# Row means by one fused VectorE instruction, and a small early load on ScalarE's queue, in a subtract-mean-and-square kernel

## The chip, the cores and the metric

One core of a Trainium2 chip. The metric is device time in microseconds (us) of one execution; the six runs of the changed kernel lie within 0.3% of each other (82.98 to 83.23).

## The reference

```python
x = np.random.randn(1024, 4096).astype(np.float32)      # axis = -1
mean = np.mean(x, axis=axis, keepdims=True)
return ((x - mean) ** 2).astype(np.float32)
```

16.78 MB are read and 16.78 MB are written.

## The kernel before

The 1024 rows are cut into two tiles. A tile has 128 partitions with four rows of 4096 fp32 each, so a partition's run is 64 KiB. All loads are issued at once, a tile is worked on in place, and one store writes it back.

```python
Q = 4
HEAD = 512
H = D * 9 // 16                                   # 2304
...
cuts = [0, HEAD, Q * D] if i == 0 else [0, Q * D]  # first tile: 2 KiB a row, then the rest
for lo, hi in zip(cuts, cuts[1:]):
    nc.sync.dma_start(out=x_tile[:, lo:hi], in_=x_t[i][:, lo:hi])
...
for i in range(ntiles):
    row = [tiles[i][:, q * D:(q + 1) * D] for q in range(Q)]
    m3 = mean_on_act(row[3])       # one ScalarE pass with accum_out
    m0 = mean_on_dve(row[0])       # reduce_sum over 4096, then a 128x1 scaling
    square_on_act(row[3], m3)
    m1 = mean_on_dve(row[1])
    square_on_act(row[0], m0)
    m2 = mean_on_dve(row[2])
    square_on_act(row[1], m1)
    square_on_act(row[2][:, :H], m2)
    back = row[2][:, H:]           # the last 1792 elements on VectorE
    nc.vector.tensor_scalar_add(out=back, in0=back, scalar1=m2)
    nc.vector.tensor_mul(out=back, in0=back, in1=back)
    nc.sync.dma_start(out=out_t[i], in_=tiles[i])
```

## Time and profile before

| what | value | how to read it |
|---|---|---|
| time | 83.23 us, median of three (83.11 to 84.35) | one of three runs was 1.3% longer |
| span of the profile | 81.4 us | the time without what lies around the program |
| VectorE, ScalarE busy | 33.4 us, 34.7 us | about 17 us for each tile |
| one large packet on each engine | 2.41 us | 1.049 MB over all 16, so 435 GB/s |
| landing of a tile to issue of its store | 17.02 us | 22.54 to 39.56 us |

The profile books the bytes of a transfer in bursts: all 16 DMA engines start a packet of 62 or 64 KiB within 0.7 us of each other in the kernel before (1.016 or 1.049 MB a burst). I give a burst's time as the mean over its bytes, from stretches of 0.05 us. The distance between two bursts is the yardstick of this document: 2.34 us within 62 KiB packets, 2.41 to 2.42 us within 64 KiB packets. Anything longer I count as lost. I call the place where the last load ends and the first store begins the first joint.

### The profile page before, as it was taken

To read this page: it belongs to the slowest core of one execution; us is meant where nothing else is said; L and a number is where in the kernel's file an instruction comes from. 1 tells how busy PE (TensorE), PEld (TensorE's weight loads), DVE (VectorE), ACT (ScalarE), POOL (GpSimd) and SP (SyncE) were. 2 spreads that over 40 slices of the span, in tenths; PEclk is the share of its full clock that TensorE was granted. 3 is DMA by queue.
4 is the path that set the end of the run, shared out by engine and by line. 5 is a ranking of instruction groups with operands and counts; after the bars stand their busy time and mean duration, and the time that the engine had idled before them with its cause. 6 is when DMAs were issued, how large, how long until landed. Compare 5 with 4: busy or idle time off the path is not lost.

```text
span 81.4 us, 83 instructions
## 1 busy us (share of the span) xinstructions
DVE 33.4 (41%) x16; ACT 34.7 (43%) x13; POOL 0.2 (0%) x4
## 2 busy tenths in 40 slices
DVE  0000000000089999999439999999900000000000
ACT  6000000000099999999339999999800000000000
POOL 0000000000000000000000000000000000000000
DMA  1999939999992999993899998399999199999290
GB/s 26 602 499 468 406 156 468 499 499 499 516 451 97 483 516 516 516 483 161 387 516 516 516 483 387 161 516 516 516 516 451 64 516 516 516 516 483 129 419 0
DMA packets 720, 33.55 MB, mean 412 GB/s; under 512 B 80, under 2 KB 80, under 8 KB 208
## 3 DMA queue, kind: packets, MB, share of 16 engines
q1 hardware_dynamic: 720, 33.55, 95.9%
HBM read 16.78 MB, written 16.78 MB: 412 GB/s over the span
## 4 chain that ended last, share of the span: by engine, by line
DMA 49%; DVE 21%; SPq 1%; issue 0%
DMA x_tile<-in_x_dram 49%; DVE neg_sum L67 16%; DVE x_tile L90 2%; DVE x_tile L89 1%; SPq L51 1%; DVE neg_mean L70 1%
## 5 line engine op out<-in xcount | busy, mean ns | idle before, releaser
L67 DVE TENSOR_REDUCE neg_sum<-x_tile 128x1 f32<-128x4096 f32 x6 | 26.5, 4412 | 25.0 <-DMA x_tile<-in_x_dram 25.0
L74 ACT ACTIVATE x_tile<-x_tile,neg_mean 128x4096 f32<-128x4096 f32 (+1 forms) x8 | 26.0, 3324 | 0.1
L59 ACT ACTIVATE copy<-x_tile 128x4096 f32<-128x4096 f32 x2 | 7.2, 3617 | 23.1 <-DMA x_tile<-in_x_dram 23.1
L90 DVE TENSOR_TENSOR x_tile<-x_tile 128x1792 f32<-128x1792 f32 x2 | 4.1, 2026 | 0.1
L89 DVE TENSOR_SCALAR x_tile<-x_tile,neg_mean 128x1792 f32<-128x1792 f32 x2 | 2.3, 1153 | 0.1
L59 ACT ACT_TABLE_LOAD x1 | 1.3, 1283 | 0.7 <-PEq L108 0.7
L70 DVE TENSOR_SCALAR neg_mean<-neg_sum 128x1 f32<-128x1 f32 x6 | 0.9, 154 | 0.2
L59 ACT ACTIVATION_READ_ACCUMULATOR copy<-x_tile 128x1 f32 x2 | 0.4, 186 | 0.0
L108 POOL MEMSET const-bfloat16-1.0<- 128x1 bf16 x1 | 0.1, 102 | 0.0
L108 POOL MEMSET const-uint8-127<- 128x1 uint8 x1 | 0.1, 101 | 0.0
L108 POOL MEMSET const-float32-0.0<- 128x1 f32 x1 | 0.1, 99 | 0.2 <-issue 0.2
L108 POOL MEMSET const-float32-1.0<- 128x1 f32 x1 | 0.1, 98 | 0.0
## 6 DMA issues: line engine op xcount, KB each, us to landing
x_tile<-in_x_dram SPq DMA_DIRECT2D x1, 7936.0 KB, 21.4
x_tile<-in_x_dram SPq DMA_DIRECT2D x1, 256.0 KB, 2.6
out_dram<-x_tile SPq DMA_DIRECT2D x2, 21.7
x_tile<-in_x_dram SPq DMA_DIRECT2D x1, 40.2
```

Of the source, the lines that this page charges most:

```text
L51: nc.sync.dma_start(out=x_tile[:, lo:hi], in_=x_t[i][:, lo:hi])
L59: nc.scalar.activation(out=copy, in_=row, func=ACT.Identity, scale=-inv_d, accum_out=neg_mean)
L67: inorder(nc.vector.reduce_sum(out=neg_sum, in_=row, axis=mybir.AxisListType.X, negate=True))
L70: inorder(nc.vector.tensor_scalar_mul(out=neg_mean, in0=neg_sum, scalar1=inv_d))
L74: inorder(nc.scalar.activation(out=part, in_=part, func=ACT.Square, bias=neg_mean, scale=1.0))
L89: nc.vector.tensor_scalar_add(out=back, in0=back, scalar1=m2)
L90: nc.vector.tensor_mul(out=back, in0=back, in1=back)
L108: nc = _bacc.Bacc("TRN2", target_bir_lowering=False, num_devices=1)
```

## The change

Its intent: fewer VectorE and ScalarE passes for the row means, and 256 KiB of the second tile loaded at the very start, on a second queue, while the first queue is only getting going. The diff, without the removed helper functions:

```diff
-    H = D * 9 // 16
+    HALF = D // 2
+    LAST = D - D // 8
...
-        cuts = [0, HEAD, Q * D] if i == 0 else [0, Q * D]
-        for lo, hi in zip(cuts, cuts[1:]):
-            nc.sync.dma_start(out=x_tile[:, lo:hi], in_=x_t[i][:, lo:hi])
+        if i == 0:
+            nc.sync.dma_start(out=x_tile[:, :HEAD], in_=x_t[i][:, :HEAD])
+            nc.sync.dma_start(out=x_tile[:, HEAD:], in_=x_t[i][:, HEAD:])
+        else:
+            end = Q * D - HEAD
+            nc.scalar.dma_start(out=x_tile[:, end:], in_=x_t[i][:, end:])
+            nc.sync.dma_start(out=x_tile[:, :end], in_=x_t[i][:, :end])
...
+        for q in range(Q):
+            row = tiles[i][:, q * D:(q + 1) * D]
+            pairs = scratch.tile([P, HALF], F32)
+            neg_mean = stats.tile([P, 1], F32)
+            inorder(nc.vector.tensor_tensor_reduce(
+                out=pairs, in0=row[:, :HALF], in1=row[:, HALF:],
+                scale=-inv_d, scalar=0.0, op0=ADD, op1=ADD, accum_out=neg_mean,
+            ))
+            cut = D if q < Q - 1 else LAST
+            nc.scalar.activation(
+                out=row[:, :cut], in_=row[:, :cut],
+                func=ACT.Square, bias=neg_mean, scale=1.0,
+            )
+            if cut < D:
+                rest = row[:, cut:]
+                nc.vector.tensor_scalar_add(out=rest, in0=rest, scalar1=neg_mean)
+                nc.vector.tensor_mul(out=rest, in0=rest, in1=rest)
```

More of the change, by code (lines that the diff above doesn't have):

```diff
@@ L12 @@
 ACT = mybir.ActivationFunctionType
+ADD = mybir.AluOpType.add
 @with_exitstack
@@ L43 @@
     scratch = ctx.enter_context(tc.tile_pool(name="scratch", bufs=1))
-    stats = ctx.enter_context(tc.tile_pool(name="stats", bufs=2 * ntiles * Q))
+    stats = ctx.enter_context(tc.tile_pool(name="stats", bufs=ntiles * Q))
     tiles = []
@@ L52 @@
         tiles.append(x_tile)
     inorder = tc.keep_in_program_order
-    def mean_on_act(row):
-        copy = scratch.tile([P, D], F32)
-        neg_mean = stats.tile([P, 1], F32)
-        nc.scalar.activation(
-            out=copy, in_=row, func=ACT.Identity, scale=-inv_d, accum_out=neg_mean
-        )
-        return neg_mean
-    def mean_on_dve(row):
-        neg_sum = stats.tile([P, 1], F32)
-        neg_mean = stats.tile([P, 1], F32)
-        inorder(nc.vector.reduce_sum(
-            out=neg_sum, in_=row, axis=mybir.AxisListType.X, negate=True
-        ))
-        inorder(nc.vector.tensor_scalar_mul(out=neg_mean, in0=neg_sum, scalar1=inv_d))
-        return neg_mean
@@ L73, in square_on_act @@
-    def square_on_act(part, neg_mean):
-        inorder(nc.scalar.activation(
-            out=part, in_=part, func=ACT.Square, bias=neg_mean, scale=1.0
-        ))
-    for i in range(ntiles):
-        row = [tiles[i][:, q * D:(q + 1) * D] for q in range(Q)]
-        m3 = mean_on_act(row[3])
-        m0 = mean_on_dve(row[0])
-        square_on_act(row[3], m3)
-        m1 = mean_on_dve(row[1])
-        square_on_act(row[0], m0)
-        m2 = mean_on_dve(row[2])
-        square_on_act(row[1], m1)
-        square_on_act(row[2][:, :H], m2)
-        back = row[2][:, H:]
-        nc.vector.tensor_scalar_add(out=back, in0=back, scalar1=m2)
-        nc.vector.tensor_mul(out=back, in0=back, in1=back)
+    for i in range(ntiles):
+        for q in range(Q):
[3 more added lines that the diff above has]
+            inorder(nc.vector.tensor_tensor_reduce(
+                out=pairs,
+                in0=row[:, :HALF],
+                in1=row[:, HALF:],
+                scale=-inv_d,
+                scalar=0.0,
+                op0=ADD,
+                op1=ADD,
+                accum_out=neg_mean,
+            ))
+            cut = D if q < Q - 1 else LAST
+            nc.scalar.activation(
+                out=row[:, :cut],
+                in_=row[:, :cut],
+                func=ACT.Square,
+                bias=neg_mean,
+                scale=1.0,
+            )
[3 more added lines that the diff above has]
+                nc.vector.tensor_mul(out=rest, in0=rest, in1=rest)
```

## The prediction

Two rates in it can be set beside the traces. ScalarE's 0.833 ns an element: before, its squares took 3698 ns for 4096 elements and 2200 ns for 2304, which is 0.836 ns. VectorE's 1 / 0.96 ns a pair: the plain tensor_tensor took 2026 ns for 1792 pairs before and 692 ns for 512 in the changed kernel, which is 1.042 ns; the two passes over those 512 elements took 0.49 and 0.69 us.

> **What bounds the kernel now.** I read the page's busy lines first. They rule out the engines: VectorE and ScalarE are each busy for about 34 us of 81.4, and both are empty for the first 22 and the last 22 us. The DMA line and the queue line point to the transfers.
>
> ```profile
> DVE 33.4 (41%) x16; ACT 34.7 (43%) x13; POOL 0.2 (0%) x4
> GB/s 26 602 499 468 406 156 468 499 499 499 516 451 97 483 516 516 516 483 161 387 516 516 516 483 387 161 516 516 516 516 451 64 516 516 516 516 483 129 419 0
> q1 hardware_dynamic: 720, 33.55, 95.9%
> ```
>
> The reader is to see one queue whose packets take 95.9% of sixteen engines' span. The dips in the GB/s row look like pauses. To settle that I cut time into 0.05 us stretches: the bytes come in bursts, one packet of 62 or 64 KB on each engine at once, 2.34 us apart in the first tile and 2.41 us apart after it, without a break from 2.7 to 77.4 us. I take the bytes to be booked when a packet starts, since the second tile's first burst (21.8 us) comes before the first tile has landed (22.5); the dips are then slices that fall between bursts. One packet per engine is 64 KiB x 16 = 1.049 MB; over 2.41 us that is 435 GB/s.
>
> The next views are the table by stretches, at the start and at the two joints (first load, second load, first store and second store follow each other on one queue), and the order of time around the first joint.
>
> ```profile
> 0.00:1.70 1.70, 0.00 (x0) 0.97 (x1) 0.20 (x4) 1.00 0.00 0
> 1.70:2.60 0.90, 0.00 (x0) 0.31 (x1) 0.00 (x0) 1.00 0.79 209
> 2.60:3.10 0.50, 0.00 (x0) 0.00 (x0) 0.00 (x0) 1.00 5.64 2179
> ...
> 38.30:39.20 0.90, 0.90 (x1) 0.90 (x1) 0.00 (x0) 1.00 2.70 1165
> 39.20:40.90 1.70, 0.30 (x1) 0.09 (x1) 0.00 (x0) 1.00 0.00 0
> 40.90:41.70 0.80, 0.00 (x0) 0.00 (x0) 0.00 (x0) 1.00 3.04 1311
> ...
> 77.20:77.90 0.70, 0.00 (x0) 0.00 (x0) 0.00 (x0) 1.00 3.45 1498
> ```
>
> ```profile
> 0.73 1.33 SPq L51 DMA_DIRECT2D x_tile<-in_x_dram  x3
> 22.54 3.62 ACT L59 ACTIVATE copy<-x_tile 128x4096 f32<-128x4096 f32 x1 [20.52 <-DMA x_tile<-in_x_dram]
> 22.61 4.42 DVE L67 TENSOR_REDUCE neg_sum<-x_tile 128x1 f32<-128x4096 f32 x1 [22.61 <-DMA x_tile<-in_x_dram]
> 26.28 13.01 ACT L74 ACTIVATE x_tile<-x_tile,neg_mean 128x4096 f32<-128x4096 f32 x4
> 37.47 2.03 DVE L90 TENSOR_TENSOR x_tile<-x_tile 128x1792 f32<-128x1792 f32 x1
> 39.56 19.64 SPq L91 DMA_DIRECT2D out_dram<-x_tile  x2
> 41.90 3.62 ACT L59 ACTIVATE copy<-x_tile 128x4096 f32<-128x4096 f32 x1 [2.61 <-DMA x_tile<-in_x_dram]
> ```
>
> The last load burst has its mean at 38.71 us and the first store burst at 41.16: 2.45 us, against 2.41 inside a transfer. The first store was issued at 39.56 and its first packets start near 41.0, about 1.45 us later. The second joint is the same (issue 58.9 us, burst 2.42 after the one before). So nothing is lost at either joint, and compute of 17.02 us a tile (22.54 to 39.56) is hidden under a transfer of 19.3 us. The margin is thin: at most 1.45 us between issue and first packet is needed and 1.45 us is there.
>
> The chain of waits says 49% DMA and 21% VectorE. Its VectorE part is the second tile's compute before the last store, but that store could not have started moving before the queue had drained at 60.4 us. Shortening that part alone buys nothing.
>
> The floor: first packets at 1.70 us, 33.55 MB at 435 GB/s is 77.1 us, and from the end of the last packet (77.4 + 2.4 = 79.8) to the span's end 1.6 us: 80.4 us against 81.4. At most 1.0 us, 1.2%, can be won by anything that leaves the bytes as they are. It lies between 1.7 and 2.6 us, where the first small load moves its 256 KiB at 209 GB/s, in 1.0 us instead of the 0.6 that the full rate would need, and in the spread of the engines.
>
> [...]
>
> **The change part by part.**
>
> The row means. Out go, per tile, three reductions of 4.41 us with a 0.15 us scaling each, and one ScalarE pass of 3.62 + 0.19 us. In come four instructions over two halves. By the trace, 2048 pairs at the tensor_tensor rate take 2026 + 256 / 0.96 = 2293 ns. Each is followed by a separate read of the accumulator, which I put at 0.15 to 0.19 us, after the tiny 0.15 us scaling and ScalarE's 0.19 us accumulator read. With a semaphore hop a row mean takes about 2.5 us, so VectorE needs 10.0 us for four.
>
> The squares. Now all on ScalarE but for 512 elements. Inside the group of four, starts are (13.01 - 2.20) / 3 = 3.60 us apart; the last, of 3584 elements, takes 2200 + 1280 x 0.833 = 3267 ns. Three starts and the last are 14.1 us. VectorE's 512 elements, about 0.5 + 0.7 us, come at 10 to 11.5 us and are hidden.
>
> So a tile's path from landing to store issue is first mean 2.5 + squares 14.1 + starts and semaphore 0.15 = 16.75 us, against 17.02: 0.27 us shorter, off the path. One trap: in the instruction order of the changed program the table load no longer runs at 0.7 us; it waits for the first tile. It takes 1.28 us while VectorE works on the first mean (2.5 us), so it is hidden[...].
>
> The early load. ScalarE's queue issues 256 KiB of the second tile at about 0.73 us, beside the first small load on the other queue. These bytes would cost 0.60 us at the full rate later, and that is saved. What they cost early is the question: if the engines fill the idle half of 1.7 to 2.6 us with them, big packets begin 0.1 to 0.2 us later and 0.4 to 0.5 us is won. If [...] each small packet keeps its 1.0 / 8 = 0.125 us of engine time, big packets begin 0.4 to 1.0 us later and the gain is from +0.2 to -0.4 us. I take a gain g of 0.2.
>
> The joint. The first tile now lands behind 256 KiB more: 22.54 + 0.6 - g = 22.94. Store one is issued at 22.94 + 16.75 = 39.69, while the queue drains at 41.1 - 0.2 = 40.9. If the issue really needs 1.45 us its packets start at 41.14 and 0.2 us is lost; if it needs the 0.97 us of the first load (issue 0.73, packets 1.70), nothing. I take 0.1 lost. At the second joint the tile lands earlier and compute is shorter, so there is no loss.
>
> Sum: 83.23 - 0.2 + 0.1 = 83.13. I say 83.1.
>
> **The rivals.** First, the half rate of the fused instruction. 2048 pairs would take about 4.4 us, a mean 4.65, and four 18.6. The last row's square could not begin before 18.6 us and would end at 21.9, so store one is issued at about 22.94 + 21.9 = 44.8 and the queue idles about 5 us at the first joint. The second tile hides most of its own delay behind the shifted store, so 88 us in all, plus 6%. [...] I give it 10%.
>
> Second, the early load only moves a cost[...]. Then 83.2 to 83.6. For it: 209 GB/s with small packets. A quarter.
>
> Third, the early load fills the hole wholly and nothing is lost at the joint: 82.7 to 82.9. A third.
>
> Fourth, faster compute shows in full, as the chain of waits with its 21% VectorE would suggest: 0.27 us or more. Against: 2.42 us at the joint, no gap to close.
>
> **Range and chances.** The middle cases give 82.7 to 83.6. One of three runs of before was 84.35, so a median can be off by some tenths; I take 82.3 to 84.2. Faster than 81.6 would need more than the whole 1.0 us: 2%. Slower than 84.9 is the half rate, with a little for what a second queue may add before the span: 9%. Within 2%: 89%.
>
> **What would show it.** Bursts 2.41 us apart through both joints, and the first large burst near 2.9 rather than 2.7 us: g is then 0.6 minus that shift. The fused instruction near 2.29 us, with a short accumulator read. Landing to store issue near 16.75 us. ScalarE's table load near 22.9 us and its first square waiting for VectorE. The prediction is wrong if the fused instruction is well over 3 us, if a burst distance at a joint is above 2.7 us, or if the first large burst comes later than 3.4 us.

## The result, and the profile after

The changed kernel takes 83.12 us (median of six, 82.98 to 83.23), the kernel before 83.28 us in the runs beside it (83.11 to 84.35). The ratio is 0.9991, with a 95% interval of 0.9974 to 1.0008. Ratios here are the mean time of one kernel's fast runs over that of the other's in the same rounds, so they are not quite the ratio of the medians. Executions over 1.5% slower than the fastest of the same kernel are left out of the means. There is no difference that these runs could show, although VectorE's work fell by 38% and ScalarE's by 15%. From the page of the changed kernel:

```profile
DVE 20.8 (26%) x20; ACT 29.4 (36%) x9; POOL 0.2 (0%) x4
...
q1 hardware_dynamic: 720, 33.29, 95.0%
q10 hardware_dynamic: 144, 0.26, 1.1%
...
L77 ACT ACTIVATE x_tile<-x_tile,neg_mean 128x4096 f32<-128x4096 f32 (+1 forms) x8 | 28.2, 3590 | 5.7 <-DVE neg_mean L66 5.7
L66 DVE CUSTOM_DVE_ANT_0 pairs<-x_tile 128x2048 f32<-128x2048 f32 x8 | 18.3, 2292 | 31.6 <-DMA x_tile<-in_x_dram 31.4
...
L66 DVE DVE_READ_ACCUMULATOR2_ANT neg_mean<- 128x1 f32 x8 | 0.7, 82 | 0.0
```

The engines do less and the queues are as full as before: 95.0% and 1.1% against 95.9%. The fused instruction takes 2292 ns for 2048 pairs, where the plain tensor_tensor took 2026 ns for 1792, so about 1.1 ns a pair in both, and its accumulator is read in 82 ns. The order of time around the first tile (start, duration, engine, line):

```profile
0.73 0.39 ACTq L56 DMA_DIRECT2D x_tile<-in_x_dram  x1
0.73 0.38 SPq L52 DMA_DIRECT2D x_tile<-in_x_dram  x1
...
23.24 1.28 ACT L77 ACT_TABLE_LOAD   x1 [23.24 <-DMA x_tile<-in_x_dram]
...
25.63 14.08 ACT L77 ACTIVATE x_tile<-x_tile,neg_mean 128x4096 f32<-128x4096 f32 x4 [1.10 <-DVE neg_mean L66]
...
39.73 18.97 SPq L88 DMA_DIRECT2D out_dram<-x_tile  x2
41.92 2.29 DVE L66 CUSTOM_DVE_ANT_0 pairs<-x_tile 128x2048 f32<-128x2048 f32 x1 [8.07 <-DMA x_tile<-in_x_dram]
```

The tile lands at 23.24 instead of 22.54 us. Its store is issued 16.49 us later, which is 0.53 us quicker than before. The second tile is there at 41.92, before it was 41.90. Now the stretches that answer to those of before (stretch, busy times, clock, DMA share, GB/s):

```profile
1.70:2.60 0.90, 0.00 (x0) 0.00 (x0) 0.00 (x0) 1.00 0.93 159
2.60:3.40 0.80, 0.00 (x0) 0.00 (x0) 0.00 (x0) 1.00 0.98 358
3.40:4.10 0.70, 0.00 (x0) 0.00 (x0) 0.00 (x0) 1.00 3.72 1586
...
38.30:39.30 1.00, 0.00 (x0) 1.00 (x1) 0.00 (x0) 1.00 2.34 1016
39.30:40.80 1.50, 0.00 (x0) 0.41 (x1) 0.00 (x0) 1.00 0.00 0
40.80:41.70 0.90, 0.00 (x0) 0.00 (x0) 0.00 (x0) 1.00 2.73 1165
```

In the kernel before, the engines moved 209 GB/s from 1.70 to 2.60 us, with one queue. With two queues they move 159 GB/s in the same stretch. The second queue did not fill the slow start. The large packets begin near 3.5 instead of 2.7 us, and the next large burst, which holds no small packets, comes at 6.01 instead of 5.43 us: 0.58 us later. The 256 KiB that are no longer loaded later are worth 0.60 us at 435 GB/s. That is the whole account of the early load: 0.60 saved, 0.58 paid. The shares of busy DMA time in these stretches, 0.79 before and 0.93 now, say that the engines were not half idle there: most of the time they were busy, at half the full rate or less. The distance at the first joint is 2.44 us, before it was 2.45.

### The profile page after: what moved, and what is told of

The parts are those of the page before. It is cut to its first block, busy times and chain, and to the rows that moved or that the text cites. A ratio compares the mean times of both kernels' runs of the same rounds, so it can differ in the third digit from the quotient of the medians.

```text
span 81.4 us, 87 instructions
## 1 busy us (share of the span) xinstructions
DVE 20.8 (26%) x20; ACT 29.4 (36%) x9; POOL 0.2 (0%) x4
## 4 chain that ended last, share of the span: by engine, by line
DMA 49%; ACT 13%; ACTq 4%; DVE 3%; SPq 1%; issue 0%
DMA x_tile<-in_x_dram 49%; ACT x_tile L77 13%; ACTq L119 4%; DVE pairs L66 3%; SPq L53 1%; SPq L52 0%; DVE neg_mean L66 0%
## 5 line engine op out<-in xcount | busy, mean ns | idle before, releaser
L77 ACT ACTIVATE x_tile<-x_tile,neg_mean 128x4096 f32<-128x4096 f32 (+1 forms) x8 | 28.2, 3590 | 5.7 <-DVE neg_mean L66 5.7
L66 DVE CUSTOM_DVE_ANT_0 pairs<-x_tile 128x2048 f32<-128x2048 f32 x8 | 18.3, 2292 | 31.6 <-DMA x_tile<-in_x_dram 31.4
L87 DVE TENSOR_TENSOR x_tile<-x_tile 128x512 f32<-128x512 f32 x2 | 1.4, 692 | 0.1
L86 DVE TENSOR_SCALAR x_tile<-x_tile,neg_mean 128x512 f32<-128x512 f32 x2 | 1.0, 488 | 0.1
L66 DVE DVE_READ_ACCUMULATOR2_ANT neg_mean<- 128x1 f32 x8 | 0.7, 82 | 0.0
```

What stands on the lines that cost most here:

```text
L66: inorder(nc.vector.tensor_tensor_reduce(out=pairs, in0=row[:, :HALF], in1=row[:, HALF:], scale=-inv_d, scalar=0.0, op0=ADD, op1=ADD, accu ...
L77: nc.scalar.activation(out=row[:, :cut], in_=row[:, :cut], func=ACT.Square, bias=neg_mean, scale=1.0,)
L86: nc.vector.tensor_scalar_add(out=rest, in0=rest, scalar1=neg_mean)
L87: nc.vector.tensor_mul(out=rest, in0=rest, in1=rest)
```

## The experiments

My theory A: a stream of packets without gaps sets the time, so neither the shorter compute nor the early load can shorten it. Its rival B: each part has an effect, and the two cancel. The twelve kernels were timed in three groups, on three chips, each beside the kernel before on the same chip. Each distance between bursts comes from one profiled run. In diffs, `-` is the kernel that is named as the base.

### Each part alone

Fused means alone: the changed kernel with the loads of before.

```diff
-        if i == 0: ... else: ...            # loads of the changed kernel, two queues
+        cuts = [0, HEAD, Q * D] if i == 0 else [0, Q * D]
+        for lo, hi in zip(cuts, cuts[1:]):
+            nc.sync.dma_start(out=x_tile[:, lo:hi], in_=x_t[i][:, lo:hi])
```

> The loads of the kernel before, the fused row means and the squares of the changed kernel. Theory A (the packets on the sixteen DMA engines set the time, compute is hidden): first store issued near 22.54 + 16.5 = 39.0 us, 0.5 us earlier than before, yet its burst stays 2.41 to 2.45 us behind the last load burst, near 41.2, and the time is that of before, ratio 0.998 to 1.002. Theory B (each part has an effect, and in the changed kernel the two cancel): the 0.5 us of shorter compute show, ratio near 0.994.

Measured: 83.21 us, ratio 0.9986 (0.995 to 1.0022). First store issued at 39.31 us (the tile landed at 22.8 in this profile), distance at the joint 2.42 us.

Early load alone: the kernel before with the loads of the changed one (the same diff the other way round).

> The loads of the changed kernel, the means and squares of the kernel before. Theory A: first large burst near 3.4 us as in the changed kernel, first tile lands near 23.2, store issued near 23.2 + 17.0 = 40.2, so its first packets start at 41.2 to 41.4 (an issue needs at most the 1.17 us that the changed kernel had); ratio 1.000 to 1.003. Theory B: the cost of the early load shows alone, about +0.5 us, ratio near 1.006.

Measured: 83.14 us, ratio 0.9979 (0.9943 to 1.0016). The second large burst came at 5.99 us, as in the changed kernel; the store was issued at 40.15 us, and the distance at the joint was still 2.42 us. So the parts don't cancel: neither ratio leaves 1 by more than its interval, some 0.4%, and both lie nominally below one, where B needs one above. An issue as late as 40.15 us cost nothing, so this issue needed less than I had allowed for: its first packets started at 41.0 us, 0.85 us later.

### The start of the stream

No small first load: the kernel before with the first tile in one piece.

```diff
-        cuts = [0, HEAD, Q * D] if i == 0 else [0, Q * D]
+        cuts = [0, Q * D]
```

> The kernel before with the first tile loaded in one piece, so no small packets at all. In before, 1.278 MB (the small load and the first large packets) take from the first packet at 1.70 us to the second large burst at 5.43 us: 3.73 us against 2.94 at 435 GB/s, 0.79 lost; the changed kernel loses 4.31 - 3.54 = 0.77 with 256 KiB more in it. Theory A (this is a fixed cost of starting the stream, no hole that small loads could fill): second burst near 1.70 + 2.41 + 0.79 = 4.9 us and the time of before, ratio 0.998 to 1.002. Theory B (small packets are slow and cause the loss): up to 0.5 us faster, ratio near 0.994. Theory C (the small load covers the preparation of the large one): slower by up to 0.5 us, ratio near 1.006.

Measured: 83.12 us, ratio 1.0002 (0.9989 to 1.0015). The second burst came at 5.04 us instead of the expected 4.9. Theories B and C of this run fall: the small load neither costs nor gains anything that can be measured.

A first load of twice the size:

```diff
-    HEAD = 512
+    HEAD = 1024
```

> The kernel before with a first load of 4 KiB a row instead of 2 KiB, so 512 KiB before the large packets on one queue, as many early bytes as the changed kernel has on two. Theory A: first and second large bursts about 0.6 us later than before, as in the changed kernel, all of it made up for by the shorter rest; ratio 0.998 to 1.002. Theory B (slow small packets): 4 KiB packets spread the cost over more bytes, up to 0.3 us faster, 0.996.

Measured: 83.33 us, ratio 1.003 (1.0012 to 1.0047), a little slower, outside what theory A had said. Second large burst at 6.03 us.

The same sum for all of them, bytes before the second large burst over 435 GB/s against the time since the first packet at 1.70 us:

| start of the stream | bytes before it, MB | at full rate, us | taken, us | lost, us |
|---|---|---|---|---|
| no small load | 1.049 | 2.41 | 3.34 | 0.93 |
| 256 KiB, one queue (before) | 1.278 | 2.94 | 3.73 | 0.79 |
| 256 + 256 KiB, two queues (changed) | 1.540 | 3.54 | 4.31 | 0.77 |
| 512 KiB, one queue | 1.507 | 3.47 | 4.33 | 0.86 |

Whatever is loaded first, and from however many queues, 0.8 to 0.9 us are lost in starting the stream. In these four starts it acts as a fixed cost and not as a hole to be filled. What the engines or the memory do in it, the runs don't show.

### No compute at all

Wrong result: the whole compute of the kernel before is taken out.

```diff
     for i in range(ntiles):
-        row = ...                          # means, squares
         nc.sync.dma_start(out=out_t[i], in_=tiles[i])
```

> Wrong result on purpose: the transfers of the kernel before with no compute at all, each store waits only for its load. Theory A: the queue order is the same and already without gaps, so the time is that of before within 0.2%, 83.1 to 83.3 us, all bursts 2.34 or 2.41 us apart. Theory B, or any theory in which compute is on the path: up to 17 us of the second tile, or at least some tenths, go away, ratio under 0.997.

Measured: 84.29 us (84.23 to 84.53), ratio 1.0116 (1.008 to 1.0153). Without any compute the kernel is 1.2% slower. No theory of mine had this. The first store is now issued at 22.68 us, and its stretches at the first joint are:

```profile
38.30:39.30 1.00, 0.00 (x0) 1.00 3.52 1049
39.30:41.90 2.60, 0.00 (x0) 1.00 0.00 0
41.90:42.90 1.00, 0.00 (x0) 1.00 2.43 1049
```

The last load burst is where it always was, at 38.8 us, but the store follows 3.52 us later. The column before the last is the share of busy DMA time. Over a stretch of 1.00 us with one packet per engine it gives a packet's own time: 3.52 us for the last load packets, 2.43 us for the first store packets. So the last load packets are recorded as taking 1.1 us longer. The second tile lands at 43.0 instead of 41.9 us.

### A store that is issued late

The changed kernel with one more ScalarE pass of 1024 or 3072 elements ahead of the last square.

```diff
+            if q == Q - 1:
+                spare = scratch.tile([P, N], F32)       # N = 1024 or 3072
+                inorder(nc.scalar.activation(out=spare, in_=row[:, :N],
+                        func=ACT.Identity, bias=neg_mean, scale=1.0))
```

> The changed kernel with one more ScalarE pass of 3072 elements before the last square of each tile, about 0.19 + 3072 x 0.833 = 2.75 us. First store issued near 39.73 + 2.75 = 42.5 instead of 39.73. Theory A with an issue-to-packet time of 1.0 to 1.17 us: the queue drains near 41.2, so 2.3 to 2.5 us are lost at the first joint and nothing at the second (the second tile has landed by then and its store is late by no more than the queue already is); ratio 1.027 to 1.031. If compute had real slack of some us beyond the joint: ratio 1.000.

Measured: 85.41 us, ratio 1.0243 (1.019 to 1.0295), a little under the 1.027 that I had said. Against the 83.25 us of the kernel before in these rounds that is 2.2 us; the distance at the joint is 4.70 us, so 2.3 us more than 2.42. In the trace of this run the extra pass takes 2.84 us, and the store is issued at 42.74 us (order of time):

```profile
42.74 0.35 SPq L94 DMA_DIRECT2D out_dram<-x_tile  x1
```

Its first packets start between 43.5 and 43.6 us (stretches):

```profile
39.40:43.40 4.00, 1.36 (x1) 3.29 (x2) 0.00 (x0) 1.00 0.00 0
43.40:43.90 0.50, 0.50 (x1) 0.00 (x0) 0.00 (x0) 1.00 4.91 2097
```

The queue was empty by then (0 GB/s from 39.40 to 43.40 us), so from this issue to its first packet it took 0.8 us. Nearly all of the delay past that shows in the time, 2.2 of 2.3 us.

> The changed kernel with one more ScalarE pass of 1024 elements per tile, about 1.0 us: first store issued near 40.75 us. In the run with 2.75 us more, the first packets came 0.8 us after the issue, so they start near 41.55 here against 41.0 when nothing is lost: 0.5 us lost, ratio near 1.005.

Measured: 83.54 us, ratio 1.0025 (0.9975 to 1.0075). Issue at 40.82, first packets at 41.65, distance 2.96 us, so half a microsecond was lost in the profiled run. The median, 0.43 us above that of before, agrees; the interval is too wide to tell it from zero.

### A store that is issued early

Is it the early issue that costs the 1.1 us? Wrong results again: the run without compute, where the first store waits for three or four ScalarE passes over its tile.

```diff
     for i in range(ntiles):
+        if i == 0:
+            for q in range(3):                         # or 4
+                row = tiles[i][:, q * D:(q + 1) * D]
+                nc.scalar.activation(out=row, in_=row, func=ACT.Identity, scale=1.0)
         nc.sync.dma_start(out=out_t[i], in_=tiles[i])
```

> Wrong result on purpose: only transfers, but the first store waits for three ScalarE passes over its tile, so it is issued near 33.2 us (22.7 in the run without compute, which lost 1.1 us at the first joint; 39.3 to 40.2 in the runs that lost nothing). If a store that is queued behind a load well before that load ends costs 1.1 us: burst distance 3.5 us at the first joint, ratio 1.012. If only the very early issue right after the first landing does it: distance 2.42, ratio 1.000.

> The same with four ScalarE passes: first store issued near 36.8 us, before the last load packets start at 38.7 us. If queueing before the last load packets have started costs 1.1 us: distance 3.5 us, ratio 1.012; if the threshold lies earlier: 2.42, ratio 1.000.

Measured: with three passes 84.83 us, ratio 1.0181 (1.0127 to 1.0235), in two groups of two runs (84.14 and 84.28; 85.39 and 85.42, of which the last counts as slow), whose split I can't explain; with four 83.89 us, ratio 1.0091 (1.0073 to 1.011). The profiled run of the four passes is the longest of its five, 84.40 us; the others lie between 83.81 and 83.89. The stores were issued at 34.38 and 38.01 us, 1.2 us later than I had said. In the trace of the three passes the table load stands in front of them: it starts at 22.44 us and takes 1.28 us, and the first pass starts at 23.73. The distances were 3.65 and 3.41 us. So the threshold lies beyond 38.0 us. But these runs have no compute in the second tile, and that could have been the cause. Three kernels with correct results test this. They start from the run with the fused means alone and divide the work better, so that a tile takes 14.8 us:

```diff
-    LAST = D - D // 8
+    LAST = D * 3 // 8          # VectorE takes 2560 elements of the last row, not 512
```

> Correct result: the loads of the kernel before, fused row means, and in the last row 2560 elements on VectorE instead of 512, so ScalarE and VectorE end together. Landing to store issue about 14.3 us instead of 16.5, first store issued near 37 us. Theory D (a store queued before the last load packets have started, at 38.4 us, costs 1.0 to 1.1 us at the joint whatever the compute): burst distance 3.4 to 3.6 us, ratio near 1.013, although compute is 2 us shorter. Theory E (the loss in the runs without full compute came from the second tile having none): distance 2.42, ratio 1.000.

Measured: 84.16 us, ratio 1.0096 (1.0042 to 1.0151); five of its six runs lie between 84.13 and 84.16, and the sixth is the slow one. Three of the eleven runs of the kernel before beside it took 83.84 to 84.08 us, the other eight at most 83.29, and no such longer run was profiled, so why it sometimes takes as long is not known; the medians are 1.05 us apart. A kernel with 1.7 us less compute a tile than the changed one is about 1 us slower. The issue of its first store, and its stretches at the joint:

```profile
37.44 0.35 SPq L84 DMA_DIRECT2D out_dram<-x_tile  x1
```

```profile
38.30:39.30 1.00, 0.00 (x0) 0.00 (x0) 0.00 (x0) 1.00 3.23 1049
39.30:41.50 2.20, 0.00 (x0) 0.00 (x0) 0.00 (x0) 1.00 0.00 0
41.50:42.70 1.20, 0.00 (x0) 0.00 (x0) 0.00 (x0) 1.00 2.02 874
```

Again the last load packets have 3.23 us each, and the first store packets 2.02 x 1.20 = 2.42 us. The control has the short compute in the second tile only:

```diff
-    LAST = D * 3 // 8
+    LASTS = [D - D // 8, D * 3 // 8]      # by tile
...
-            cut = D if q < Q - 1 else LAST
+            cut = D if q < Q - 1 else LASTS[i]
```

> The same with the short compute in the second tile only; the first tile keeps the split of the changed kernel, its store is issued near 39.2 us. Theory D: no loss, distance 2.42 to 2.45, ratio 0.998 to 1.002. If short compute as such were the cause: ratio near 1.013 or 1.006.

Measured: 83.3 us, ratio 1.0001 (0.9949 to 1.0053). Issue at 39.18 us, and the last load packets are back at 2.43 us (the issue, then the stretches):

```profile
39.18 17.97 SPq L84 DMA_DIRECT2D out_dram<-x_tile  x2
...
38.30:39.30 1.00, 0.00 (x0) 0.85 (x1) 0.00 (x0) 1.00 2.43 1049
39.30:40.80 1.50, 0.00 (x0) 0.00 (x0) 0.00 (x0) 1.00 0.00 0
40.80:41.90 1.10, 0.00 (x0) 0.00 (x0) 0.00 (x0) 1.00 2.21 953
```

So it is not the short compute of the second tile. The short compute of the first tile is what moves its store's issue. That the issue, and not this compute as such, is the cause is supported by the runs without squares and means, which lose as much at issues from 22.68 to 38.01 us; the direct test, short compute with its store held back to 39.5 us, was not run. Last, the short compute in both tiles with the first store on the other queue:

```diff
-        nc.sync.dma_start(out=out_t[i], in_=tiles[i])
+        queue = nc.scalar if i == 0 else nc.sync
+        queue.dma_start(out=out_t[i], in_=tiles[i])
```

> The kernel with the short compute in both tiles, but the first store goes out on ScalarE's queue, so it does not stand behind the load in one queue. If the loss of theory D belongs to the order inside one queue: load and store packets mix from about 37.5 us, the second tile lands 1 to 2 us later, the second store still finds the engines busy, ratio 0.998 to 1.003. If it belongs to the change from loading to storing on the engines whatever the queue: ratio near 1.013 again.

Measured: 85.08 us, ratio 1.0225 (1.0166 to 1.0285). The loss at the joint is there on another queue too (3.48 us), so it does not come from standing behind the load in one queue. This run loses more than the joint explains: the second tile lands at 45.5 us, its store is issued only at 60.29, and there is a further 0.3 us at the second joint (a distance of 2.68 us). The load of the second tile landed 43.9 us after its issue, against 40.2 us in the kernel before; what delayed it is not shown. The profiled run, 84.78 us, is the shortest of the six; what lengthens the others I did not follow up.

All runs in the order of the first store's issue:

| first store issued, us | run | distance at the joint, us | ratio to before |
|---|---|---|---|
| 22.68 | no compute | 3.52 | 1.0116 |
| 34.38 | three passes | 3.65 | 1.0181 |
| 37.39 | short compute, other queue | 3.48 | 1.0225 |
| 37.44 | short compute | 3.24 | 1.0096 |
| 38.01 | four passes | 3.41 | 1.0091 |
| 39.18 | short compute, second tile only | 2.42 | 1.0001 |
| 39.31 | fused means alone | 2.42 | 0.9986 |
| 39.53 | no small load | 2.42 | 1.0002 |
| 39.56 | before | 2.45 | 1 |
| 39.60 | first load of 512 KiB | 2.49 | 1.003 |
| 39.73 | changed | 2.44 | 0.9991 |
| 40.15 | early load alone | 2.42 | 0.9979 |
| 40.82 | 1024 elements more | 2.96 | 1.0025 |
| 42.74 | 3072 elements more | 4.70 | 1.0243 |

(The distances are means over all sixteen engines; in the runs at 38.01, 39.18 and 39.31 one of them has its first store packet about half a microsecond after the mean.) The last load packets start between 38.4 and 39.3 us in all of these runs. Between 38.0 and 39.2 lies the lower edge of a window; its upper edge I estimate from where the queue drains, near 41.1, less the 0.8 us that the issues at 40.82 and 42.74 took, so near 40.3. In the seven runs that issue inside it less than 0.1 us is lost (distances of 2.42 to 2.49 us). Before and changed kernel both issue inside it. What holds the last load packets for a microsecond when a store is already queued, I can only guess at, and leave open. It is not seen at the second joint: in the run without compute the second store is issued about 18 us ahead of the end of the first store, and the distance there is 2.42 us. Nor is it seen between the two loads: in the kernel before the second load is issued some 18 us ahead of the last packets of the first, and the distance there is 2.35 us.

None of the kernels with a correct result was faster than the kernel before by more than its interval.

## Why the prediction was right or wrong

The time was right, 83.1 predicted and 83.12 measured, and so was its main reason. Two terms of the sum were mis-sized, in opposite directions. That the figures meet within 0.02 us is luck: the median of the kernel before alone moved from 83.23 us of three runs to 83.28 of six. So is the issue of the first store, 39.69 us predicted and 39.73 measured: the tile landed 0.30 us later than predicted, and its path to the store was 0.26 us shorter.

- **The bound.** Right: bursts 2.41 us apart through both joints, 2.44 at the first. Half a microsecond less compute (fused means alone) gave 0.9986, not distinguishable from 1. The fourth rival, that the chain of waits with its 21% VectorE shows a gain to be had, falls.
- **"The margin is thin".** Wrong in its size and its side. On a queue that had drained, an issue took 0.8 us to its first packet (42.74 to between 43.5 and 43.6 us; the first load of the program took 0.97, from 0.73 to 1.70). From this I estimate that the kernel before had about 0.65 us to spare against being late (39.56 + 0.8 = 40.4, against 41.0). The edge I did not see is the other one: in the five runs with an issue at 38.0 us or earlier the distance was 0.8 to 1.2 us longer.
- **"Shortening that part alone buys nothing".** Right: it was said of the second tile's compute, and with that alone shortened to 14.7 us the ratio was 1.0001. What the prediction did not see is that the same cut in the first tile too costs 1% (1.0096).
- **The fused instruction.** 2293 ns predicted, 2292 measured. The half rate of the first rival was a supposition: no instruction of this kind is in the trace of before. The rival, with its 88 us, falls.
- **The row mean, 2.5 us.** It was 2.34 us (from 23.29 to 25.63): the accumulator read takes 82 ns and begins before the main instruction's record ends (25.51 against 25.58 us), where I had put 0.15 to 0.19 us and a hop. With that, the path from landing to store is 16.49 and not 16.75 us.
- **The table load.** It ran when the first tile landed, as said (at 23.24 us, 22.9 predicted), took 1.28 us, and the first square started 1.11 us after its end, as VectorE's mean came. It cost nothing.
- **The early load, g = 0.2.** The step that failed. The argument was that engines were half idle from 1.7 to 2.6 us and that a second queue would use some of it. The prediction read this from the rate, 209 of 435 GB/s; the column beside it in the same line, the share of busy DMA time, has 0.79. With two queues the share was 0.93, that stretch moved 159 GB/s instead of 209, the stream was 0.58 us later for 0.60 saved, and g is 0.02. The second rival, that the load only moves its cost, was nearest; I had given it a quarter. Its reason, slow small packets, is not enough: without any small packets the time was the same, 1.0002. The third rival, that the hole is filled wholly, had been given a third and falls. The prediction's own sign of being wrong, a first large burst later than 3.4 us, did come: the burst has its mean at 3.67 us, 0.86 later than before. By its rule (0.6 minus that shift) g would be -0.26, but the first burst is a poor yardstick: in the kernel before its packets were slow too (2.62 us to the next burst instead of 2.34), so the second burst is used here.
- **The joint, 0.1 lost.** Measured none: 2.44 against 2.45 us. With g this makes 83.23 - 0.02 - 0 = 83.21 in place of 83.13, and the measured difference to before, 0.9991 with 0.17% to either side, can't tell these apart.
- **Small misreadings.** The bursts of the first tile are not all 2.34 us apart: the first two are 2.62 us apart. At 209 GB/s, 256 KiB would take 1.25 us and not 1.0; the stretch of 0.9 us holds 188 KB of it. ScalarE is not empty for the first 22 us: its table load runs from 0.73 us for 1.28 us, which costs nothing there.

## What to carry to other kernels

In the kernel before and in the changed one the bursts followed each other 2.34 to 2.45 us apart, without gaps, from the second large one to the last. What was lost lay at the start (0.77 to 0.93 us in four starts) and, in some runs of the experiments, at the first joint (up to 2.3 us), and half a microsecond less compute gave a ratio of 0.9986, although the chain of waits had 21% VectorE. In a kernel whose trace looks like this, count what is lost at the start and at each joint between transfers before expecting anything from engine time. Before taking work away from an engine that feeds a store, look at when that store will then be issued: here a store that was queued before the last load packets had started cost about 1 us, so faster compute of the first tile made a slower kernel (1.0096). A small load put on a second queue at the start was no gift of time here: it saved the 0.60 us that its own bytes take at the full rate, and delayed the large packets by 0.58.
